# Output projections as seven quarter products in a two-layer encoder kernel

## The chip, the cores and the metric

The kernel runs on one core of a Trainium2 chip. A core has TensorE (matrix products, PE in the profile; PEld is its loading of the stationary operand), VectorE (DVE), ScalarE (ACT), GpSimd (POOL) and SyncE (SP), which here only issues DMAs. Matrix products read SBUF and write PSUM; the dense phase of this kernel keeps eight PSUM tiles of 128 x 512 fp32, here called banks. ScalarE and GpSimd issue DMAs too. Each engine runs its own instructions in program order and waits for other engines by semaphores. The metric is the device time of one execution in microseconds; lower is better.

## What is computed

The reference is a trunk of two layers over 1024 tokens of width 1024. Layer 0 mixes the tokens by neighbourhood attention (mixer A), layer 1 by grouped-query attention (mixer B). After each mixer stand the output projection, the residual sum, and a gate projection:

```python
def reference(x, p, norm_g, a_w_in, a_rpb, a_w_out, b_w_in, ..., ple_norm_g, ple_w_gate, ple_w_proj, final_norm_g):
    for i in range(DEPTH):                      # DEPTH = 2
        h = rms_norm(x, norm_g[i])
        if i % NUM_MIXERS == 0:
            y = mixer_a(h, a_w_in[j], a_rpb[j], a_w_out[j])
        else:
            y = mixer_b(h, b_w_in[j], b_q_norm[j], b_k_norm[j], b_w_out[j])
        x = x + y
        g = jax.nn.sigmoid(rms_norm(x, ple_norm_g[i]) @ ple_w_gate[i])
        x = x + g * (p[i] @ ple_w_proj[i])
    return rms_norm(x, final_norm_g)
```

Both mixers end in `(o * silu(gate)) @ w_out`, with `w_out` of 1024 x 1024. That last product, once per layer, is the output projection. In the kernel `y` names its left operand, `o * silu(gate)`.

## The kernel before, in words

**Numbers in halves.** Every fp32 operand of a product is held as two tiles of type fp32r, a high part (ScalarE's copy) and a low part (VectorE's difference). A product is three matmuls into the same PSUM bank: high x high, high x low, low x high (`split3`, L314; its matmuls stand in the profile under L315, in `mm`). A transpose is a matmul against `ident`.

**Operands.** The left operand of all dense products lies in `HTh` and `HTl`: token tile t (8 tiles of 128), channel chunk k (8 of 128), channels on the partitions. Weights come in units of 128 x 1024 fp32 (512 KB). The class `Weights` (`WQ`) keeps one queue of units: `stage` issues their loads on SP into one of two `wstage` buffers (L208), `pump`, called once per step of work, makes the high half on ScalarE (L225) and the low half on VectorE (L230, one step later). Each unit has a pool number: pool 1 has four slots that live throughout, pool 2 has four in the dense phase alone. `hold` names the unit at which staging stops, `age` and `lag` are the steps that a unit waits.

**Mixers.** Attention of 16 heads, in order, with the dense products of the next heads woven in (`mix`). `post` and `later` are lists of functions that fall due after so many steps. Two heads make a pair; when both heads of a pair are done for a token half `hf` (tiles 0 to 3, or 4 to 7), `head_end` yields `fin`: y of that pair, 128 channels x 512 tokens in the tile `Y`. For pairs 0 to 6 it is multiplied on GpSimd (L529, L530), then after `YS` = 11 steps split into halves (L526, L527), and two steps later both halves are stored to DRAM, `yD` (L522). During the last heads `load_y` (L279) brings channel chunks 0 to 6 of a tile back into `HTh` and `HTl`. The last pair goes straight there by `fin_last` (Y final at L512, halves at L515, L516). `pp_items` makes `p @ ple_w_proj` at the end of a mixer and stores it to `ppD` (L568).

**Dense phase** (`dense_phase`, L1232 on), per layer. Two kinds, `out` (output projection) and `ple` (gate projection), each for two column halves `hf` of 512, each for 8 token tiles. A tile and half is 8 chunks x 3 = 24 matmuls of 128 x 512 into one bank, written as two parts of 4 chunks. For `out` and `hf` = 0, the first parts of tiles 0 to 3 run first, since they need only pairs 0 to 3. The result is added to the residual `X` by VectorE (L1286); `X` is loaded by SP (L1344) and stays in SBUF. In the second half, each finished tile is squared and summed by ScalarE (L1369, the first half at L1360), every two tiles VectorE makes the root (`norm_r`, L426 and `rsqrt`, L326 to L334) and the scaled rows `xn` (L1382), and `pend_ht`, called once per part, transposes half a tile of them on TensorE into `HTh` and `HTl` (`to_ht`, L443 to L445) for the gate projection. There, ScalarE's tanh (L1278) and two VectorE operations (L1279, L1280) add the gated term to `X`, with `pp` tiles loaded back by SP (L1334). `rope_tables` (L1387 to L1402), called in layer 0 in the `out` half 0 at tile 4, prepares the rotary tables for mixer B: GpSimd multiplies, SP stores.

**Order of the work.** It is written out by hand: each engine runs its instructions in the order in which the Python code issues them. Nothing is reordered later; only the waits for data and for buffers are added.

## Time and profile before

| | |
|---|---|
| median of 3 runs | 1550.73 us (1549.6 to 1550.89) |
| span of the profiled execution | 1548.4 us; its whole time isn't listed apart from the runs |
| TensorE busy | 1521.1 us, 98% of the span |
| VectorE, ScalarE, GpSimd busy | 1016.2, 874.1, 280.4 us |
| output projection of layer 0 | 529.2 to 616.2 us |
| output projection of layer 1 | 1355.7 to 1442.7 us |
| moved by DMA | 138.32 MB, 89 GB/s in the mean |

How to read the lines of the profile: a group is "line, engine, operation, output <- inputs, shape, xcount | busy us, mean ns of one | idle time of the engine just before, and what ended it". A line of the timeline is "start, duration, engine, line, operation, names, xcount [idle time before it <- what ended that]"; `SPq` is a DMA's issue on SP. In the table by stretch, each engine has its busy time and its number of instructions, then come the granted TensorE clock (1.00 is full), the busy share of the DMA engines and GB/s. Matmuls are pipelined: one of 128 x 512 has a duration of some 390 ns, but the next begins after about 227.

### The profile page before, as it was taken

How to read it: one execution, taken by the hardware profiler on the slowest of the kernel's cores; microseconds unless marked ns; L12 is line 12 of the kernel's file. 1: busy time of each engine (PE TensorE's matmuls, PEld its weight loads, DVE VectorE, ACT ScalarE, POOL GpSimd, SP SyncE). 2: the span in 40 equal slices, each digit the busy share in tenths (PEclk: the TensorE clock that was granted, in tenths of full speed). 3: DMA queues.
4: the chain of work that ended last, by engine and by line, in shares of the span. 5: the costliest groups of instructions: out<-in, count | busy, mean ns of one | idle time of the engine just before them, and what ended most of it. 6: DMA issues, size and time to landing. Idle time of an engine off the chain costs nothing.

```text
span 1548.4 us, 24286 instructions
## 1 busy us (share of the span) xinstructions
PE 1521.1 (98%) x9072; PEld 1328.5 (86%) x9072; DVE 1016.2 (66%) x1990; ACT 874.1 (56%) x1757; POOL 280.4 (18%) x380
## 2 busy tenths in 40 slices
PE   8999999999999999999999999999999999999997
PEld 8888988988988888888988889989999888788886
DVE  7666576576477436557877776777777877625636
ACT  6565465465466522333567776767767767622422
POOL 1221121121121010000312122444131200000022
PEclk9999999999999999999999999999999999999999
DMA  8212122122033961232210111111101123651213
GB/s 263 97 40 72 60 80 61 52 82 79 35 99 97 355 232 55 79 139 78 75 48 22 38 48 50 41 38 56 57 27 42 62 62 116 224 197 55 74 54 131
DMA packets 90005, 138.32 MB, mean 89 GB/s; under 512 B 17056, under 2 KB 56096, under 8 KB 89888
## 3 DMA queue, kind: packets, MB, share of 16 engines
q1 hardware_dynamic: 87296, 129.17, 25.6%
q10 hardware_dynamic: 2592, 7.61, 1.4%
q8 instruction: 71, 1.16, 0.3%
q14 instruction: 46, 0.38, 0.1%
HBM read 104.13 MB, written 36.15 MB: 91 GB/s over the span
## 4 chain that ended last, share of the span: by engine, by line
PE 41%; DVE 7%; ACT 3%; issue 2%; DMA 0%; SPq 0%; ACTq 0%; DVEq 0%
PE d L315 22%; PE o L315 7%; PE t L1144 6%; PE s L315 5%; DVE PTl L1147 2%; DVE mn L1128 1%; ACT PTh L1146 1%; ACT P L1134 1%; PE t L443 1%; DVE QS L1108 1%; DVE wl L230 0%; PE t L1098 0%; DVE t L962 0%; DVE qt L963 0%; DVE Y L459 0%
## 5 line engine op out<-in xcount | busy, mean ns | idle before, releaser
L315 PE MATMUL d<-wh,HTh 128*128 128x256 f32 (+1 forms) x1096 | 369.3, 339 | 3.6 <-ACT HTh L444 1.3
L315 PE MATMUL d<-wh,HTl 128*128 128x256 f32 (+1 forms) x1096 | 363.2, 333 | 0.3 <-DVE HTl L445 0.3
L315 PE MATMUL d<-wl,HTh 128*128 128x256 f32 (+1 forms) x1096 | 362.6, 333 | 0.0
L1147 DVE TENSOR_TENSOR PTl<-t,PTh 128x512 fp32r<-128x512 f32 x256 | 164.4, 684 | 110.1 <-ACT PTh L1146 109.7
L315 PEld LDWEIGHTS d<-wh,HTh 128*128 128x128 f32 x1096 | 206.4, 189 | 26.6 <-ACT HTh L444 1.6
L315 PEld LDWEIGHTS d<-wl,HTh 128*128 128x128 f32 x1096 | 206.7, 189 | 21.7
L315 PEld LDWEIGHTS d<-wh,HTl 128*128 128x128 f32 x1096 | 206.5, 189 | 22.0 <-DVE HTl L445 0.5
L315 PE MATMUL d<-HTh,wh 128*128 128x512 f32 x504 | 205.8, 408 | 0.0
L315 PE MATMUL d<-HTh,wl 128*128 128x512 f32 x504 | 198.1, 393 | 0.0
L315 PE MATMUL d<-HTl,wh 128*128 128x512 f32 x504 | 197.5, 392 | 0.0
L1134 ACT ACTIVATE P<-s,mn 128x1024 f32<-128x1024 f32 x128 | 142.8, 1115 | 57.2 <-DVE mn L1128 56.3
L1146 ACT ACTIVATE PTh<-t 128x512 fp32r<-128x512 f32 x256 | 140.2, 594 | 45.4 <-PE t L1144 44.8
L1128 DVE TENSOR_REDUCE mn<-s 128x1 f32<-128x1024 f32 x128 | 154.8, 1209 | 11.7 <-PE s L315 11.6
L1144 PE MATMUL t<-ident,P 128*128 128x128 f32 x1024 | 137.7, 275 | 6.4 <-DVE PTl L1147 4.4
L230 DVE TENSOR_TENSOR wl<-wstage,wh 128x1024 fp32r<-128x1024 f32 x86 | 110.2, 1285 | 40.1 <-ACT wh L225 39.6
L1144 PEld LDWEIGHTS t<-ident,P 128*128 128x128 f32 x1024 | 114.6, 140 | 22.5 <-DVE PTl L1147 16.6
L315 PE MATMUL s<-KA,QS 128*128 128x512 f32 (+2 forms) x384 | 133.5, 402 | 0.0
L315 PE MATMUL s<-KB,QS 128*128 128x512 f32 (+2 forms) x384 | 121.7, 371 | 0.0
L315 PE MATMUL o<-PTh,V 128*128 128x256 f32 (+2 forms) x672 | 118.8, 288 | 1.2 <-DVE Y L459 0.9
L315 PE MATMUL o<-PTl,V 128*128 128x256 f32 (+2 forms) x672 | 119.0, 288 | 0.1
L695 DVE TENSOR_TENSOR PTl<-t,PTh 128x384 fp32r<-128x384 f32 (+1 forms) x128 | 66.6, 520 | 74.7 <-ACT PTh L694 73.4
L315 PEld LDWEIGHTS d<-HTh,wl 128*128 128x128 f32 x504 | 94.6, 188 | 21.7
(201 smaller groups left out, 2486.0 us busy)
## 6 DMA issues: line engine op xcount, KB each, us to landing
wstage<-in_wts SPq DMA_DIRECT2D x92, 512.0 KB
pp<-ppD SPq DMA_DIRECT2D x32, 256.0 KB
X<-in_x SPq DMA_DIRECT2D x15, 512.0 KB
rb<-rD SPq DMA_DIRECT2D x56, 128.0 KB
ppD<-th SPq DMA_DIRECT2D x20, 256.0 KB
xD<-X SPq DMA_DIRECT2D x8, 512.0 KB
X<-xD SPq DMA_DIRECT2D x8, 512.0 KB
yD0h<-rb SPq DMA_DIRECT2D x14, 256.0 KB
```

Source lines behind the costliest of these rows:

```text
L230: eng.tensor_tensor(lo[:, c:c + n], s[:, c:c + n], hi[:, c:c + n], ALU.subtract)
L315: pe.matmul(ps, a, b, start=first, stop=last, skip_group_check=True)
L443: pe.transpose(ps[:, k], xn[:, (4 * c + k) * 128:(4 * c + k + 1) * 128], ident)
L695: dve.tensor_tensor(PTl[:, sl], ps[:, :m], PTh[:, sl], ALU.subtract)
L1108: post.add(DQ, lambda: dve.tensor_tensor(qs[oth], raw[own], qs[own], ALU.subtract))
L1128: dve.tensor_reduce(mn, ps, axis=AX.X, op=ALU.min)
L1134: act.activation(p, ps, AF.Exp, bias=mn, scale=-1.0, accum_out=RS[h, hf][:, t:t + 1])
L1144: pe.transpose(ps[:, i], p[:, k * 128:(k + 1) * 128], ident)
L1146: act.activation(PTh[:, ks, c], ps, AF.Copy)
L1147: dve.tensor_tensor(PTl[:, ks, c], ps, PTh[:, ks, c], ALU.subtract)
```

## The change

Both output projections are made from seven products of quarter matrices instead of eight, in Winograd's form. Call the quarters of y A11 (tiles 0 to 3, chunks 0 to 3), A12 (tiles 0 to 3, chunks 4 to 7), A21, A22 (tiles 4 to 7), and of the weights B11, B12 (column halves of the first 512 rows), B21, B22. The new function `strassen_out` runs, in blocks of 12 matmuls (one tile, 4 chunks, 3 terms):

- P1 = A11 B11 (4 blocks, one for each tile), P2 = A12 B21 (4);
- S2 T2 (4), S3 T3 (4), A22 T4 (4), added onto P1 in the same PSUM banks, and read out by VectorE (`fold`) after each block;
- S1 T1 (4) and Q4 B22 (4), interleaved, in new banks.

Here T3 = B22 + B12, T2 = T3 + B11, T4 = T2 + B21, T1 = B11 + B12; S1 = A21 - A22, S3 = A11 - A21, S2 = S1 - A11, Q4 = A12 + S2. The quarters of X get their products from `fold`, `first` (P2) and `second` (P1, copied out by ScalarE) with the signs that this form needs.

The weight sums: two 512 KB tiles `SM` are loaded with B22 by SP, and GpSimd's queue issues DMAs that add B12, then B11, then B21 onto them in SBUF (`plus`), each after the halves of the sum so far are made (`wh`, `wl`). For T1 they are loaded again. The input sums are VectorE's, on fp32 quarters that SP fetches (`fetch_a`) from a new DRAM copy of y, `yF`. The mixers store it: `whole` after 11 steps, the last pair in `fin_last`. The halves `yD` are still made for tiles 0 to 3 and, of tiles 4 to 7, for chunks 4 to 6, now 4 steps after `whole`. The list `todo` says after which block each of these steps is issued.

Beside this, the gate weights of half 0 are staged only from the first block of the last eight on (`hold`), those of half 1 go to pools 4 and 2; the squares, roots and scaled rows are made in pairs of tiles (m, 4 + m) during the last eight blocks, with the buffers `sb` and the gains opened there; the gate projection's first half runs in the order 0, 4, 1, 5, 2, 6, 3, 7; and `rope_tables` moves to the end of that half.

```diff
+    yF = [dram.tile([NT, 128, 8, 128], F32, name=f"yF{l}") for l in range(2)]
...
+    WQ.hold = ("ple", 0, 0, 0)
...
-        for n in ("out", "ple"):
-            for hf in range(2):
-                q.extend([((n, l, hf, u), 1 + hf) for u in range(4)])
+        q.extend([(("out", l, 0, u), 1) for u in range(4)])
+        q.extend([(("ple", l, 0, u), 1) for u in range(4)])
+        q.extend([(("ple", l, 1, u), 4 - u // 2 * 2) for u in range(4)])
 
     def load_y(l, t):
         for d, src in zip((HTh, HTl), yD[l]):
-            (act if t < 4 else sync).dma_start(d[:, t, 0:7].bitcast(F32), src[t, :, 0:7])
+            k0 = 4 if t >= 4 else 0
+            (act if t < 4 else sync).dma_start(d[:, t, k0:7].bitcast(F32), src[t, :, k0:7])
...
+            sync.dma_start(yF[layer][ts, :, 7, :].rearrange("t p c -> p t c"), y3)
...
-            def store(c, src):
-                sync.dma_start(yD[layer][c][4 * hf:4 * hf + 4, :, pair, :].rearrange("t p c -> p t c"),
+            def store(dst, src):
+                sync.dma_start(dst[4 * hf:4 * hf + 4, :, pair, :].rearrange("t p c -> p t c"),
                                src.rearrange("p (t c) -> p t c", t=4))
 
             def split():
                 act.activation(yhi, Y, AF.Copy)
                 dve.tensor_tensor(ylo, Y, yhi, ALU.subtract)
-                post.add(2, lambda: (store(0, rb), store(1, Y)))
+                post.add(2, lambda: (store(yD[layer][0], rb), store(yD[layer][1], Y)))
+
+            def whole():
+                store(yF[layer], Y)
+                if pair >= 4 or hf == 0:
+                    post.add(4, split)
             pool.tensor_tensor(Y, Y, G, ALU.mult)
             pool.tensor_tensor(Y, Y, rb, ALU.mult)
-            post.add(YS[layer], split)
+            post.add(YS[layer], whole)
...
+    def strassen_out(l, X, ps_d, ps_t):
+        xs = x if l == 0 else xD
+        es = ExitStack()
+        scr = es.enter_context(tc.tile_pool(name="scr", bufs=1))
+        todo = {}
+
+        q11, q21 = [("out", l, 0, 0), ("out", l, 0, 1)], [("out", l, 0, 2), ("out", l, 0, 3)]
+        q12, q22 = [("out", l, 1, 0), ("out", l, 1, 1)], [("out", l, 1, 2), ("out", l, 1, 3)]
+        W = {"b11": [WQ.get(k) for k in q11], "b21": [WQ.get(k) for k in q21]}
+        SM = [scr.tile([128, 1024], F32, name=f"sum{u}") for u in range(2)]
+        raw = {}
+        P1 = [None] * 4
+        A = {n: [scr.tile([128, 4, 128], F32, name=n, bufs=4) for m in range(4)] for n in ("a21", "a22", "a11", "a12")}
+
+        def load(dst, key):
+            sync.dma_start(dst, wts[UNIT[key]])
+
+        def plus(u, keys):
+            pool.dma_start(SM[u], wts[UNIT[keys[u]]], accum_op=ALU.add)
+
+        def halves(name, u, pid, src):
+            def hi():
+                W.setdefault(name, [None, None])[u] = WQ.alloc[pid]()
+                act.activation(W[name][u][0], src(), AF.Copy)
+
+            def lo():
+                w = W[name][u]
+                dve.tensor_tensor(w[1], src(), w[0], ALU.subtract)
+            return hi, lo
+
+        H = {(n, u): halves(n, u, pid, lambda n=n, u=u: raw[u] if n == "b22" else SM[u])
+             for n, pid in (("t3", 2), ("t2", 1), ("t4", 1), ("t1", 1), ("b22", 2)) for u in range(2)}
+
+        def wh(n, u):
+            H[n, u][0]()
+
+        def wl(n, u):
+            H[n, u][1]()
+
+        def fetch_a(n, m):
+            t, c = {"a21": (4, 0), "a22": (4, 1), "a11": (0, 0), "a12": (0, 1)}[n]
+            sync.dma_start(A[n][m], yF[l][t + m, :, 4 * c:4 * c + 4])
+
+        def sums(m):
+            a21, a22, a11 = (A[n][m] for n in ("a21", "a22", "a11"))
+            dve.tensor_tensor(a22, a21, a22, ALU.subtract)
+            dve.tensor_tensor(a21, a11, a21, ALU.subtract)
+            dve.tensor_tensor(a11, a22, a11, ALU.subtract)
+
+        def q4(m):
+            dve.tensor_tensor(A["a12"][m], A["a12"][m], A["a11"][m], ALU.add)
+
+        PLACE = {"s2": ("a11", 4, 0), "s3": ("a21", 0, 0), "s1": ("a22", 0, 1), "q4": ("a12", 4, 0)}
+
+        def sh(n, m):
+            src, t, c = PLACE[n]
+            act.activation(HTh[:, t + m, 4 * c:4 * c + 4], A[src][m], AF.Copy)
+
+        def sl(n, m):
+            src, t, c = PLACE[n]
+            w = slice(4 * c, 4 * c + 4)
+            dve.tensor_tensor(HTl[:, t + m, w], A[src][m], HTh[:, t + m, w], ALU.subtract)
+
+        def first(m):
+            fold(m, 0, P2[m], ALU.add)
+
+        def second(m):
+            xt = X[m][:, 0:512]
+            dve.tensor_tensor(xt, xt, P1[m], ALU.add)
+
+        for u in range(2):
+            load(SM[u], q22[u])
+        for u in range(2):
+            plus(u, q12)
+        for n in ("a21", "a11", "a22"):
+            for m in range(4):
+                fetch_a(n, m)
+        todo[1] = [lambda: sums(0)]
+        todo[2] = [lambda: sh("s2", 0), lambda: sums(1), lambda: wh("t3", 0), lambda: wh("t3", 1)]
+        todo[3] = [lambda: sl("s2", 0), lambda: wl("t3", 0), lambda: wl("t3", 1), lambda: sh("s2", 1),
+                   lambda: plus(0, q11), lambda: plus(1, q11)]
+        todo[4] = [lambda: sl("s2", 1), lambda: sums(2)] + [lambda t=t: sync.dma_start(X[t], xs[t]) for t in range(4)]
+        todo[5] = [lambda: sums(3), lambda: sh("s2", 2), lambda: sh("s2", 3)]
+        todo[6] = [lambda: sl("s2", 2), lambda: sl("s2", 3), lambda: wh("t2", 0), lambda: wh("t2", 1)]
+        todo[7] = [lambda: wl("t2", 0), lambda: wl("t2", 1), lambda: plus(0, q21), lambda: plus(1, q21)]
+        todo[7] += [lambda m=m: fetch_a("a12", m) for m in range(4)]
+        todo[8] = [lambda: sh("s3", 0), lambda: sh("s3", 1), lambda: sl("s3", 0), lambda: sl("s3", 1)]
+        todo[8] += [lambda t=t: sync.dma_start(X[t], xs[t]) for t in range(4, 8)]
+        todo[9] = [lambda: sh("s3", 2), lambda: sh("s3", 3), lambda: sl("s3", 2), lambda: sl("s3", 3)]
+        todo[10] = [lambda: wh("t4", 0), lambda: first(0), lambda: first(1), lambda: q4(0), lambda: q4(1)]
+        todo[11] = [lambda: wh("t4", 1), lambda: wl("t4", 0), lambda: first(2), lambda: first(3)]
+        todo[12] = [lambda: wl("t4", 1), lambda: load(SM[0], q11[0]), lambda: load(SM[1], q11[1]),
+                    lambda: plus(0, q12), lambda: plus(1, q12), lambda: q4(2), lambda: q4(3)]
+        todo[13] = [lambda: sh("s1", 0), lambda: sh("s1", 1), lambda: second(0), lambda: sl("s1", 0), lambda: sl("s1", 1)]
+        todo[14] = [lambda: sh("s1", 2), lambda: sh("s1", 3), lambda: second(1), lambda: sl("s1", 2), lambda: sl("s1", 3)]
+        todo[15] = [lambda: sh("q4", 0), lambda: sh("q4", 1), lambda: second(2), lambda: sl("q4", 0), lambda: sl("q4", 1)]
+        todo[16] = [lambda: wh("t1", 0), lambda: sh("q4", 2), lambda: sh("q4", 3), lambda: second(3)]
+        todo[17] = [lambda: wl("t1", 0), lambda: wh("t1", 1), lambda: sl("q4", 2), lambda: sl("q4", 3)]
+        todo[18] = [lambda: wl("t1", 1), lambda: wh("b22", 0)]
+        todo[19] = [lambda: wl("b22", 0), lambda: wh("b22", 1)]
+        todo[20] = [lambda: wl("b22", 1)]
+
+        def fetch_raw(u):
+            raw[u] = stg.tile([128, 1024], F32, name="wstage")
+            load(raw[u], q22[u])
+        todo[14] += [lambda: fetch_raw(0), lambda: fetch_raw(1)]
+
+        def block(ps, t, c, wk, start):
+            for k in range(4):
+                wh, wl = W[wk][k // 2]
+                cc = slice((k % 2) * 512, (k % 2) * 512 + 512)
+                split3(ps, HTh[:, t, 4 * c + k, :], HTl[:, t, 4 * c + k, :], wh[:, cc], wl[:, cc],
+                       start and k == 0, k == 3)
+
+        def fold(t, c, ps, op):
+            xt = X[t][:, 512 * c:512 * c + 512]
+            if op is ALU.subtract:
+                dve.tensor_tensor(xt, xt, ps, op)
+            else:
+                dve.tensor_tensor(xt, ps, xt, op)
+
+        Y, P2 = [None] * 4, [None] * 4
+        clock = [0]
+
+        def pulse():
+            for f in todo.pop(clock[0], ()):
+                f()
+            clock[0] += 1
+
...
+        for wk, t0, c, xt0, xc, op in (("t2", 4, 0, 0, 1, ALU.subtract), ("t3", 0, 0, 4, 1, ALU.subtract),
+                                       ("t4", 4, 1, 4, 0, ALU.add)):
+            for m in range(4):
+                block(Y[m], t0 + m, c, wk, False)
+                fold(xt0 + m, xc, Y[m], op)
+                pulse()
+        WQ.live[1] += 2
+        WQ.live[2] += 2
+        for kind, m in ((5, 0), (5, 1), (3, 0), (5, 2), (3, 1), (5, 3), (3, 2), (3, 3)):
+            if kind == 5:
+                Y[m] = ps_d.tile([128, 512], F32, name="d")
+                block(Y[m], m, 1, "t1", True)
+                fold(4 + m, 1, Y[m], ALU.add)
+            else:
+                block(Y[m], 4 + m, 0, "b22", False)
+                fold(m, 1, Y[m], ALU.add)
+            pulse()
...
+            yield kind, m
...
+            ready = []
+            squared = []
+
+            def roots(n):
+                if squared and squared[0][0] < n:
+                    m = squared.pop(0)[1]
+                    sm = ss[:, 2 * m:2 * m + 2]
+                    r = sb.tile([128, 2], F32, name="rn", bufs=4)
+                    wk = sb.tile([128, 8], F32, name="wkn", bufs=2)
+                    dve.tensor_scalar(sm, sm, 0.5 / D, 0.5 * EPS, op0=ALU.mult, op1=ALU.add)
+                    rsqrt(r, sm, wk)
+                    ready.append(((m, 4 + m), r))
+
+            def scale_pair():
+                if not ready or len(pend) > 4:
+                    return
+                ts, r = ready.pop(0)
+                xs = []
+                for i, t in enumerate(ts):
+                    xn = xalloc()
+                    dve.scalar_tensor_tensor(xn, X[t], r[:, i:i + 1], g1, op0=ALU.mult, op1=ALU.mult)
+                    xs.append(xn)
+                pend.extend([(clock[0] + 3, t, xn, (c,)) for c in range(2) for t, xn in zip(ts, xs)])
+
+            for n, (step, m) in enumerate(strassen_out(l, X, ps_d, ps_t)):
+                if n == 0:
+                    sb = es.enter_context(tc.tile_pool(name="dsb", bufs=2))
+                    wp4 = es.enter_context(tc.tile_pool(name=f"wp4{l}", bufs=2))
+                    WQ.alloc[4] = lambda: [wp4.tile([128, 1024], F32R, name=f"w{c}4") for c in "hl"]
+                    WQ.cap[4] = 2
+                    WQ.hold = ("bg", 0) if l == 0 else None
+                    g1 = load_gain(sb, 2 * l + 1, 2)
+                    g2 = load_gain(sb, 2 * l + 2, 2)
+                    junk = sb.tile([128, D], BF16, name="junk", bufs=1)
+                    ss = sb.tile([128, 8], F32, name="ssn", bufs=1)
+                    WQ.age, WQ.lag, age, lag = 2, 0, WQ.age, WQ.lag
+                if step == 5:
+                    act.activation(junk, X[4 + m], AF.Square, accum_out=ss[:, 2 * m + 1:2 * m + 2])
+                else:
+                    act.activation(junk, X[m], AF.Square, accum_out=ss[:, 2 * m:2 * m + 1])
+                    squared.append((n, m))
+                WQ.pump()
+                roots(n)
+                pend_ht()
+                scale_pair()
+            WQ.age, WQ.lag = age, lag
...
+                    seq = list(range(NT)) if hf else [0, 4, 1, 5, 2, 6, 3, 7]
...
+                    order = [(t, i) for t in seq for i in range(2)]
+                    if hf == 0:
+                        order = [(t, i) for p in range(4) for i in range(2) for t in seq[2 * p:2 * p + 2]]
...
-                        if l == 0 and kind == "out" and hf == 0 and t == 4:
+                        if l == 0 and hf == 0 and t == seq[-1]:
...
+        hg = sb.tile([128, 512], F32, name="th")
         sync.dma_start(hg[:, :256], bcast(hgains, 0, 256))
+        pool.tensor_scalar(hg[:, :128], hg[:, :128], -0.125, None, op0=ALU.mult)
```

76 lines of the change are left out of this document (40 added, 36 removed).

## The prediction

> **What bounds the kernel now.** I read the page first (busy shares, the span in slices), then busy time by stretch over the two output projections, then the timelines of each engine where they begin.
>
> ```profile
> span 1548.4 us, 24286 instructions
> ...
> PE 1521.1 (98%) x9072; PEld 1328.5 (86%) x9072; DVE 1016.2 (66%) x1990; ACT 874.1 (56%) x1757; POOL 280.4 (18%) x380
> ```
> ```profile
> core 0: us, PE busy (x) PEld busy (x) DVE busy (x) ACT busy (x) POOL busy (x), PEclk, DMA share, GB/s
> 529.20:616.20 87.00, 86.92 (x395) 71.28 (x396) 43.08 (x77) 25.15 (x49) 5.50 (x4) 1.00 0.50 170
> 1355.70:1442.70 87.00, 86.94 (x395) 71.31 (x396) 37.05 (x71) 23.66 (x47) 0.00 (x0) 1.00 0.31 112
> ...
> 529.28:551.05 21.77, 21.77 (x96) 18.03 (x97) 9.38 (x11) 6.45 (x10) 0.00 (x0) 1.00 0.89 331
> 1355.76:1377.50 21.74, 21.74 (x96) 18.02 (x97) 6.25 (x7) 6.52 (x11) 0.00 (x0) 1.00 0.66 253
> ```
>
> TensorE is the bound: 98% of the span, and in both output projections (87 us each) without a gap. So removed matmuls pay in full, provided that the new operands are there in time. The price is in the third and fourth rows: 96 matmuls of 128x512 take 21.77 us, 0.227 us each. I call 12 of them (one tile, four k-chunks, three high/low terms) a block: 2.72 us.
>
> **The gain.** An output projection has 8 tiles, 2 column halves, 8 k-chunks, 3 terms: 384 matmuls, 32 blocks. Seven quarter products have 7 x 4 = 28 blocks, 336 matmuls. Over two layers 96 go, which is just the window above: -21.8 us.
>
> **Start of the Strassen stage.** P1 (A11 B11) and P2 (A12 B21) need nothing new, so they start as now and cover 8 blocks, 21.8 us. The ninth block, S2 T2, needs S2 from three fetched quarters and T2 from two accumulations in a row. When can that be?
>
> ```profile
> 529.28 0.50 PE L315 MATMUL d<-wh,HTh 128*128 128x512 f32 x1 [0.74 <-ACT G L567]
> ...
> 532.12 0.69 DVE L512 TENSOR_TENSOR Y<-Y,t 128x512 f32<-128x512 f32 x1
> 533.51 0.69 DVE L516 TENSOR_TENSOR HTl<-Y,HTh 128x512 fp32r<-128x512 f32 x1 [0.70 <-ACT HTh L515]
> 534.12 2.36 DVE L230 TENSOR_TENSOR wl<-wstage,wh 128x1024 fp32r<-128x1024 f32 x2
> ...
> 535.40 0.33 SPq L208 DMA_DIRECT2D wstage<-in_wts  x1
> 535.97 0.81 SPq L419 DMA_DIRECT2D gain<-in_gains  x2
> 536.82 1.43 SPq L1344 DMA_DIRECT2D X<-in_x  x3
> ...
> 538.91 1.06 ACT L225 ACTIVATE wh<-wstage 128x1024 fp32r<-128x1024 f32 x1 [4.48 <-DMA wstage<-in_wts]
> 544.39 0.69 DVE L1286 TENSOR_TENSOR X<-d,X 128x512 f32<-128x512 f32 x1 [3.16 <-DMA X<-in_x]
> ...
> 539.00:545.00 6.00, 6.00 (x28) 4.99 (x27) 1.83 (x2) 0.97 (x1) 0.00 (x0) 1.00 1.01 369
> 1364.00:1370.00 6.00, 6.00 (x28) 4.95 (x28) 0.31 (x1) 0.00 (x0) 0.00 (x0) 1.00 1.02 415
> ```
>
> The last pair's Y is final at 532.81, when P1 has run 3.5 us. Only then can SP store it to yF, and behind that store in SP's order stand both SM loads and twelve fetches. A lone 512 KB load lands 3.5 us after its issue (535.40 to 538.91). The fourth 512 KB of a queue lands after 9.0 us (535.40 to 544.39). With the DMA full (share 1.01, 1.02) it moves 369 to 415 GB/s. SM (1 MB), a21 and a11 (2 MB) and the first tile of a22 (0.25 MB) are 3.25 MB: 9.0 us for 2 MB and 3.5 for the rest at 369 is 12.5; at 400 GB/s behind 2.2 us of latency it is 10.7, and up to 2.7 more where the accumulations share the engines. From 533.5 that gives 544 to 547; I take T = 546.
>
> From T the new order on VectorE decides, which runs in order. A 128x512 costs 0.62 back to back (533.51 to 534.12), a 128x1024 1.18 (2.36 for two). Ahead of the first T2 low half stand four `sums` of three (2.0 each, 8.0), four `sl` of S2 (2.5), two low halves of T3 (2.4): 12.9; with that half itself 14.1. ScalarE must form S2 high and then T2 high in the same order, and ends beside it. So the ninth block starts at 560.1 where PE is ready at 551.05: 9.0 us of stall.
>
> In layer 1 the order is kinder:
>
> ```profile
> 1353.43 0.69 DVE L512 TENSOR_TENSOR Y<-Y,o 128x512 f32<-128x512 f32 x1
> ...
> 1346.31 9.75 SPq L568 DMA_DIRECT2D ppD<-th  x3
> 1358.04 0.81 SPq L419 DMA_DIRECT2D gain<-in_gains  x2
> ...
> 1355.76 0.50 PE L315 MATMUL d<-wh,HTh 128*128 128x512 f32 x1 [0.73 <-ACT th L567]
> ```
>
> Y is final at 1354.12, but SP is held by the ppD stores to 1356.1, and memory of the mixer may hold the loads to 1358.0, as it does the gains now. With 12.5 us T is 1368.6 to 1370.4; at 1369.5 the ninth block starts at 1383.6, due 1377.5: 6.1 us. Lower bound of both: a store and a fetch at 3 us each with nothing before them, T 538.9 and 1362: stalls 1.9 and 0. Upper: T 5 us later, 14 and 11.
>
> **The accumulating DMAs.** The trace has none. Nearest row: the plain load, 3.5 us; if source, destination and result each move at the plain rate behind two latencies, about 8.3. T3 low is done 5.8 after T and T2 high cannot start before 12.1, so 6.3 us are free. I take 6 (it reads and writes, so nearer the upper end): hidden. At 8.3, with a second one behind it, 3 more per layer. Not below zero: nothing else now makes these sums. Behind a late one on POOL stand only its fellows; on ScalarE, though, the P1 and S copies, and on VectorE every fold. The Trainium skill, DMA: Bandwidth & Descriptors, section Anatomy of one DMA — SWDGE (gpsimd) path, fits 2.0 us plus bytes at 436 GB/s, an estimate of 3.2 us for each; the sum would be the same by it. It is not a fit for accumulation, and no run here shows one.
>
> **Middle.** In blocks 9 to 18 VectorE has 10 folds, 12 `sl`, 4 `q4`, 8 `first`/`second` (34 x 0.62 = 21.1) and 3 `wl` (3.5): 24.6 in 27.2 us, and a fold may be three blocks late before PE waits for its bank. No cost. T4's accumulation is issued at T + 15 and needed at T + 36. T1's is tighter: SM is free again when T4 low is done, about T + 32, so load (3.5) and accumulation (6) are in at T + 42, its halves at T + 44, and PE wants them at T + 47. That holds, with 3 us to spare.
>
> **Tail into the gate projection.** Square, norm, scaling and gate weights, spread over the second column half now (half of 87 us), fall on the last eight blocks.
>
> ```profile
> 585.89 0.16 DVE L426 SCALAR_TENSOR_TENSOR stn<-sq 128x2 f32<-128x2 f32 x1 [0.85 <-ACT xn L1369]
> ...
> 588.12 2.48 DVE L1382 SCALAR_TENSOR_TENSOR xn<-X,stn,gain 128x1024 f32<-128x1024 f32 x2
> ...
> L444 ACT ACTIVATE HTh<-t 128x512 fp32r<-128x512 f32 x64 | 37.2, 593 | 47.8 <-PE t L443 47.6
> L225 ACT ACTIVATE wh<-wstage 128x1024 fp32r<-128x1024 f32 x89 | 92.9, 1051 | 9.2 <-DMA wstage<-in_wts 8.4 <-DVE HTl L516 0.8
> L736 ACT ACTIVATE junk<-X 128x1024 bf16<-128x1024 f32 x7 | 7.4, 1056 | 0.9 <-DMA X<-in_x 0.9
> L736 ACT ACTIVATION_READ_ACCUMULATOR junk<-X 128x1 f32 x7 | 1.4, 198 | 0.0
> ```
>
> A root is eleven small operations, 2.2 us (585.89 to 588.12), a pair's scaling 2.4. From the end of the fourth of the eight blocks VectorE has fold, `wl`, root, scaling (6.4), then fold and `wl` (1.8), then fold, root, scaling (5.2), then the next fold (0.6): 14.0. ScalarE's square waits for that fold (1.25), then a weight half (1.05), then HTh of tile 0 (0.6): ready at 16.9. PE has four blocks and two transpose groups to do, 11.6: stall 5.3, and about 1 more at tile 4. Take 6 per layer. Bounds 2 (if the square slips ahead) and 9 (gate weights late behind the two gain loads moved in front of them).
>
> **Clock.**
>
> ```profile
> 1540.00:1544.00 4.00, 0.21 (x2) 0.01 (x1) 3.72 (x14) 3.41 (x6) 0.00 (x0) 0.95 0.02 8
> 1544.00:1548.40 4.40, 0.00 (x0) 0.00 (x0) 0.00 (x0) 0.00 (x0) 0.00 (x0) 0.50 0.59 233
> ```
>
> After PE's last matmul, at 1540.2, the granted clock is 0.95 over four us, then 0.50: it halves after some 3.6 us of idling. The return isn't shown. If it takes one block, a stall costs 1.4 more. Both starts are well above 3.6 us, the tails (5.3) only just, so I count them as one: three, 4 us. Bounds 0 and 8. The Trainium skill, TensorE: Matmul & The Clock Gate, section Part 1: The HAM clock gate, has the same fall after about 3.4 us (the rows agree) and a return after about 3.4 us of work, an estimate of 1.7 us a stall; by it the three cost 5.
>
> **At nothing.** The yF stores (16 a layer for 8 yD stores fewer) lie under mixers whose DMA is a quarter used:
>
> ```profile
> 400.00:500.00 100.00, 99.86 (x560) 86.70 (x560) 66.35 (x143) 61.38 (x134) 19.93 (x22) 1.00 0.26 78
> ...
> 551.32 1.62 SPq L1391 DMA_DIRECT2D xn<-in_rope  x1
> 561.19 2.48 SPq L1402 DMA_DIRECT2D ropeD<-xn  x4
> ```
>
> Splits come four ticks later and VectorE's in-place half must now wait for the yF store to have read Y; 0 to 2 us in all. The shorter loads of y gain nothing, PE waits for none. The rotary tables, moved to the end of the gate's first half, hold SP some 10 us (551.32 to 561.19), and behind them the two pp loads: the first gate evacuation waits 7 us, covered by four PSUM banks (21.8 us): 0 to 2.
>
> **Sum.** -21.8 + 9.0 + 6.1 + 12 + 4 = +9.3 us. On the span that is 1557.7; the runs' median (1550.73) is 2.3 above the span, so 1560.0.
>
> **Rivals.** (1) Preparation keeps up, the other side: SP's fetches overtake or T comes 5 us earlier, and the square slips ahead in the tail. Stalls 4 + 1 + 2 x 3, no clock loss: -10.8, 1540. For it: VectorE works only 9.4 of the first 21.8 us. Against: the DMA share there is 0.89 already, while 8 MB (SM and its first two sums 3, quarters of y 3, X 2) are to come in that time. It decides where all stalls stay under 21.8 us. Chance 0.25. (2) Slow accumulations, deciding from 6.3 us each on: at 12 us T2 comes 6 us later and T1 3 us, at 15 us 9 and 6, per layer; with 13 us, +20 on the forecast, 1580. For it: they meet a DMA that is full in these stretches. Against: the plain load beside them takes 3.5. Chance 0.18. (3) Gain and stalls cancel, 1551: chance 0.07. Forecast, 1554 to 1572 of its own: 0.50.
>
> Faster by over 0.2% (3 us, what this measurement can tell) 0.25, within 0.07, slower 0.68. The range leaves a tenth out at each end: 1541 to 1580.
>
> **What would show it.** 336 matmuls for 384 in each projection; PE idle before the ninth block, released by ScalarE's or VectorE's T2 half, 9 and 6 us; T3 halves ready long before use; a second gap at the gate's first tile, released by HTh L444; granted clock under 1 behind the gaps. Wrong if the ninth block follows without a gap, or if the gap hangs on a POOL DMA.

## The result, and the profile after

The changed kernel is slower: 1597.24 us median (1595.54 to 1598.76) against 1550.16 us (1548.95 to 1550.89) for the kernel before on the same chip, a ratio of 1.0307 (95% interval 1.0292 to 1.0321). The forecast was 1560.0, with a range of 1541 to 1580: the sign was right, the size was not. The profiled execution has a span of 1594.6 us, 46.2 more than before.

First the page of the changed kernel (busy time and DMA issues), and then the group of its first-term matmuls from the answer by lines.

```profile
PE 1515.1 (95%) x8976; PEld 1317.7 (83%) x8976; DVE 1076.4 (68%) x2079; ACT 897.0 (56%) x1769; POOL 297.1 (19%) x397
...
sum<-in_wts POOLq DMA_DIRECT2D x16, 512.0 KB, 8.8
```

```profile
L317 PE MATMUL d<-wh,HTh 128*128 128x256 f32 (+1 forms) x1032 | 349.4, 340 | 45.8 <-ACT wh L1263 32.7 <-ACT HTh L446 10.3 <-ACT G L575 0.7
```

The 96 matmuls are gone (8976 for 9072), but PE is busy for 95% of a longer span and not 98%. The last line has PE's busy time and mean, and behind the second bar the idle time just before these matmuls and what ended it: 32.7 us for ScalarE's weight half at L1263, 10.3 for the transposed tile at L446. The accumulating DMA, which no trace had shown, takes 8.8 us from issue to landing.

The same idle times in order, from PE's timeline (start, duration, what ran, in brackets the idle time ahead and who ended it):

```profile
534.43 0.50 PE L317 MATMUL d<-wh,HTh 128*128 128x512 f32 x1 [0.74 <-ACT G L575]
...
573.94 0.79 PE L317 MATMUL d<-wh,HTh 128*128 128x512 f32 x1 [17.44 <-ACT wh L1263]
...
639.45 0.50 PE L317 MATMUL d<-wh,HTh 128*128 128x512 f32 x1 [4.38 <-ACT HTh L446]
715.33 0.98 PE L445 MATMUL t<-ident,xn 128*128 128x128 f32 x4 [3.86 <-DVE xn L1596]
...
1421.49 0.80 PE L317 MATMUL d<-wh,HTh 128*128 128x512 f32 x1 [15.26 <-ACT wh L1263]
...
1488.11 0.80 PE L317 MATMUL d<-wh,HTh 128*128 128x512 f32 x1 [4.37 <-ACT HTh L446]
```

The first row is the first block of layer 0: it starts at 534.43, where the kernel before had 529.28, so the first mixer has already lost 5.2 us. Then come the ninth block of layer 0 (17.44 us late), the gate (4.38), the gate's second half (3.86), and the ninth block and the gate of layer 1 (15.26, 4.37).

Behind the gaps PE is slow as well. The rows are, in this order, the first eight blocks of layer 0, the 10.88 us from the ninth block on (the time of four blocks at full speed) in layer 0, the gate's first block in layer 0, and then the stretches behind the ninth block and at the gate in layer 1:

```profile
core 0: us, PE busy (x) PEld busy (x) DVE busy (x) ACT busy (x) POOL busy (x), PEclk, DMA share, GB/s
534.43:556.20 21.77, 21.77 (x96) 17.94 (x96) 4.94 (x6) 4.68 (x7) 1.95 (x2) 1.00 0.79 236
...
573.94:584.82 10.88, 9.89 (x26) 6.73 (x27) 4.38 (x6) 4.46 (x7) 1.71 (x2) 0.61 0.86 178
...
639.45:644.16 4.71, 4.71 (x13) 3.37 (x14) 4.36 (x15) 1.63 (x3) 0.00 (x0) 0.64 0.52 185
...
1421.49:1432.37 10.88, 9.91 (x21) 6.68 (x22) 4.32 (x5) 4.59 (x7) 1.71 (x2) 0.50 0.83 168
...
1488.11:1493.40 5.29, 5.29 (x13) 4.03 (x14) 4.91 (x17) 1.63 (x3) 0.00 (x0) 0.50 0.54 196
```

Behind the ninth blocks PE completed 26 and 21 matmuls where 48 fit, at a granted clock of 0.61 and 0.50: 22 and 27 matmuls of 0.227 us, 5.0 and 6.1 us, are lost a second time. At the gates 12 matmuls (the rows count the start of one more) took 4.71 and 5.29 us where a block at full speed takes 2.72: 2.0 and 2.6 us.

With that, nearly all of the 46.2 us has a place: -21.8 for the matmuls, +5.2 in the first mixer, +32.7 in the waits ahead of the ninth blocks, +11.1 in the blocks behind them, +8.8 in the waits at the two gates, +4.6 in the slow blocks behind these, and +5.2 at the gate's second half in layer 0 (3.86 and the clock behind it; the 5.2 is what the run below that removes it gains). That makes 45.8; the remaining 0.4 us is not assigned.

### The profile page after: what moved, and what is told of

The parts are those of the page before. It is cut to its first block, busy times and chain, and to the rows that moved or that the text cites. A ratio compares the mean times of both kernels' runs of the same rounds, so it can differ in the third digit from the quotient of the medians.

```text
span 1594.6 us, 24337 instructions
## 1 busy us (share of the span) xinstructions
PE 1515.1 (95%) x8976; PEld 1317.7 (83%) x8976; DVE 1076.4 (68%) x2079; ACT 897.0 (56%) x1769; POOL 297.1 (19%) x397
## 3 DMA queue, kind: packets, MB, share of 16 engines
q0 software_dynamic: 2304, 8.39, 2.8%
## 4 chain that ended last, share of the span: by engine, by line
PE 37%; DVE 7%; ACT 4%; issue 3%; DMA 1%; POOL 0%; ACTq 0%; DVEq 0%; POOLq 0%
PE d L317 19%; PE o L317 7%; PE t L1152 6%; PE s L317 5%; DVE PTl L1155 2%; DMA sum<-in_wts 1%; DVE mn L1136 1%; ACT P L1142 1%; ACT PTh L1154 1%; DVE wl L231 1%; PE t L445 0%; DVE QS L1116 0%; PE t L1106 0%; DVE t L970 0%; DVE xn L1456 0%
## 5 line engine op out<-in xcount | busy, mean ns | idle before, releaser
L317 PE MATMUL d<-wh,HTh 128*128 128x256 f32 (+1 forms) x1032 | 349.4, 340 | 45.8 <-ACT wh L1263 32.7
L317 PE MATMUL d<-wl,HTh 128*128 128x256 f32 (+1 forms) x1032 | 342.4, 334 | 1.9 <-DVE wl L1267 1.9
L317 PE MATMUL d<-wh,HTl 128*128 128x256 f32 (+1 forms) x1032 | 342.1, 333 | 1.0 <-DVE HTl L447 1.0
L317 PEld LDWEIGHTS d<-wh,HTh 128*128 128x128 f32 x1032 | 197.5, 192 | 69.1 <-ACT wh L1263 35.1
L317 PEld LDWEIGHTS d<-wl,HTh 128*128 128x128 f32 x1032 | 197.7, 192 | 22.6 <-DVE wl L1267 3.9
L317 PEld LDWEIGHTS d<-wh,HTl 128*128 128x128 f32 x1032 | 197.5, 192 | 21.5 <-DVE HTl L447 3.2
L1136 DVE TENSOR_REDUCE mn<-s 128x1 f32<-128x1024 f32 x128 | 154.9, 1210 | 12.3 <-PE s L317 12.2
L231 DVE TENSOR_TENSOR wl<-wstage,wh 128x1024 fp32r<-128x1024 f32 x78 | 98.4, 1265 | 26.6 <-ACT wh L226 26.3
```

Source lines behind the costliest of these rows:

```text
L231: eng.tensor_tensor(lo[:, c:c + n], s[:, c:c + n], hi[:, c:c + n], ALU.subtract)
L317: pe.matmul(ps, a, b, start=first, stop=last, skip_group_check=True)
L1136: dve.tensor_reduce(mn, ps, axis=AX.X, op=ALU.min)
```

## The experiments

All kernels were patched from the changed one. Their times are of one execution each, so they are compared by stages of the trace: in the six executions whose first mixer is that of the changed kernel, the first block of layer 0 stood between 534.4 and 538.5, and a few us of the time are that alone.

### The first mixer: when the split may overwrite Y

VectorE overwrites Y with its low half, and must now wait until the yF store has read it. In the changed kernel (SP's and VectorE's rows):

```profile
192.42 0.54 SPq L525 DMA_DIRECT2D yF<-Y  x1
...
195.54 1.08 DVE L530 TENSOR_TENSOR Y<-Y,rb 128x512 fp32r<-128x512 f32 x1 [2.77 <-DMA yF<-Y]
```

The first edit gave the store 8 steps of work (ticks) instead of 4:

```diff
-                    post.add(4, split)
+                    post.add(8, split)
...
-            post.add(YS[layer], whole)
+            post.add(YS[layer] - 4, whole)
```

> The split of a pair comes 8 ticks after its yF store was issued and not 4, with the store 4 ticks earlier, so the split stands where it stood. Theory (VectorE's in-place half waits until the yF store has read Y, and the mixer's exponentials behind it run late): the first layer's projection starts near 529.5 again (534.4 with the change, 529.3 before), the wait of the split on yF<-Y is gone, and the time falls by 5 us, to 1592. Rival (the sixteen more stores load the queue whenever they stand): the start stays near 534 and the time at 1597.

It took 1598.75 us, with the first block at 535.49. The rows of this kernel say why the edit did nothing:

```profile
191.90 0.60 SPq L470 DMA_DIRECT2D rb<-rD  x1
192.60 0.54 SPq L525 DMA_DIRECT2D yF<-Y  x1
...
195.73 1.13 DVE L530 TENSOR_TENSOR Y<-Y,rb 128x512 fp32r<-128x512 f32 x1 [2.86 <-DMA yF<-Y]
```

The store was asked for earlier and went out at the same moment, 192.60: it stands in SP's order behind the loads of rb, and these wait for the row sums. The wait on the split is the same, 2.86 us. So the run neither bore out my expectation nor tested the rival; the distance in ticks was the wrong quantity. The second edit took the store out of SP's order:

```diff
             pool.tensor_tensor(Y, Y, rb, ALU.mult)
-            post.add(YS[layer], whole)
+            ts = slice(4 * hf, 4 * hf + 4)
+            pool.dma_start(yF[layer][ts, :, pair, :].rearrange("t p c -> p t c"), Y.rearrange("p (t c) -> p t c", t=4))
+            if pair >= 4 or hf == 0:
+                post.add(YS[layer], split)
```

> POOL stores yF itself, right after its last multiplication of a pair, instead of SP 11 ticks later behind its waits for the row sums, and the split stands at 11 ticks as before the change. Theory (the in-place split waits for a yF store that SP can only issue behind the loads of rb): the split's waits on yF<-Y are gone and the first projection starts at 529 to 530.5 (534.4 to 536.8 in the runs with the change, 529.3 before); the time is 1590 to 1593. Rival (the bytes or the number of the stores, wherever they are issued): the start stays at 534 or later and the time at 1596 or more.

1588.94 us. The first block starts at 529.54, as in the kernel before (529.28):

```profile
529.54 0.50 PE L317 MATMUL d<-wh,HTh 128*128 128x512 f32 x1 [0.74 <-ACT G L574]
```

VectorE's waits on `yF<-Y` in the first mixer, 3.3 us in the changed kernel, are gone. The bytes and the number of the stores are the same, so the loss of 5 us (up to 9 in other executions) did not come from them. It came with the place of the store in SP's order and with the split, which the change had put 4 ticks later; the edit takes both back, and no run separates the two.

### The start: the accumulation, the order, and where they meet

The start of layer 0 in the changed kernel, from the timelines of SP, POOL, VectorE and ScalarE:

```profile
537.99 0.37 SPq L517 DMA_DIRECT2D yF<-Y  x1
...
540.56 0.82 SPq L1255 DMA_DIRECT2D sum<-in_wts  x2
...
545.34 1.95 POOL L1258 DMA_DIRECT2D sum<-in_wts  x2 [51.89 <-DMA sum<-in_wts]
...
558.13 0.69 DVE L1285 TENSOR_TENSOR a<-a,a 128x512 f32<-128x512 f32 x1 [16.51 <-DMA a<-yF]
...
564.37 0.86 POOL L1258 DMA_DIRECT2D sum<-in_wts  x1 [17.08 <-DVE wl L1267]
...
572.83 1.06 ACT L1263 ACTIVATE wh<-sum 128x1024 fp32r<-128x1024 f32 x1 [2.26 <-DMA sum<-in_wts]
```

SP may load SM 2.6 us after the last yF store was issued. The first tile of a22 is there 17.6 us after that (558.13), and VectorE's order then puts two sums and T3's low halves ahead of the second accumulation (564.37), which lands 8.5 us later and is what the ninth block waits for. Two experiments took one link each.

```diff
-            pool.dma_start(SM[u], wts[UNIT[keys[u]]], accum_op=ALU.add)
+            pool.dma_start(SM[u], wts[UNIT[keys[u]]])
```

> The accumulating DMAs become plain copies, so the weight sums are left out (the output is not the reference's). Theory (two accumulations of 8.8 us in a row hold T2): each copy lands 3.5 to 5 us after its issue, the stall ahead of the ninth block falls from 17.4 and 15.3 us to 11 to 13 and 9 to 11, the short waits behind it go, and the time falls by 12 to 16 us, to 1581 to 1585. Rival (the quarters of y and VectorE's order alone set that moment): the stall stays above 16 us and the time within 3 us of 1597.

1586.5 us. The ninth blocks wait 13.02 and 10.79 us, 4.4 and 4.5 less. That is the upper end of what I expected (11 to 13 and 9 to 11), and the time is 1.5 us above my range: a plain copy issued by POOL in this place still takes 7.1 us and not 3.5 to 5.

```profile
556.98 0.69 DVE L1285 TENSOR_TENSOR a<-a,a 128x512 f32<-128x512 f32 x1 [13.38 <-DMA a<-yF]
...
571.50 0.80 PE L317 MATMUL d<-wh,HTh 128*128 128x512 f32 x1 [13.02 <-ACT wh L1263]
```

And from its page, DMA issues:

```profile
sum<-in_wts POOLq DMA_DIRECT2D x16, 512.0 KB, 7.1
```

SM was issued at 542.55 here, so a22 came 14.4 us later and not 17.6: accumulating, for plain copying of the same bytes, also slows the fetches, by some 3 us. What accumulating costs is this part; the greater part of the stall would be there with plain copies.

```diff
-        todo[1] = [lambda: sums(0)]
-        todo[2] = [lambda: sh("s2", 0), lambda: sums(1), lambda: wh("t3", 0), lambda: wh("t3", 1)]
-        todo[3] = [lambda: sl("s2", 0), lambda: wl("t3", 0), lambda: wl("t3", 1), lambda: sh("s2", 1),
-                   lambda: plus(0, q11), lambda: plus(1, q11)]
+        todo[1] = [lambda: wh("t3", 0), lambda: wh("t3", 1)]
+        todo[2] = [lambda: wl("t3", 0), lambda: wl("t3", 1), lambda: plus(0, q11), lambda: plus(1, q11),
+                   lambda: sums(0)]
+        todo[3] = [lambda: sh("s2", 0), lambda: sums(1), lambda: sl("s2", 0), lambda: sh("s2", 1)]
```

> T3's halves and the accumulation behind them (for T2) are issued ahead of the input sums on ScalarE, VectorE and POOL. Theory (VectorE's order: the sums of the quarters wait for the last fetch and T3's low halves stand behind them): POOL issues the accumulations for T2 near 557 instead of 564.4, the ninth block starts 6 to 8 us earlier (stall 9 to 11 us in the first layer, 8 to 10 in the second) and the time falls by 12 to 16 us, to 1581 to 1585. Rival (a full DMA: the accumulations would only move into the stretch of the fetches and take longer there, or S2 would be late instead): stall 15 us or more, time 1593 or more.

1587.81 us, between the two. In layer 0 of this kernel:

```profile
556.69 1.06 ACT L1263 ACTIVATE wh<-sum 128x1024 fp32r<-128x1024 f32 x1 [12.90 <-DMA sum<-in_wts]
...
559.31 0.86 POOL L1258 DMA_DIRECT2D sum<-in_wts  x1 [9.99 <-DVE wl L1267]
...
562.11 0.68 DVE L1285 TENSOR_TENSOR a<-a,a 128x512 f32<-128x512 f32 x1
...
572.36 1.99 ACT L1263 ACTIVATE wh<-sum 128x1024 fp32r<-128x1024 f32 x2
573.45 0.79 PE L317 MATMUL d<-wh,HTh 128*128 128x512 f32 x1 [14.88 <-ACT wh L1263]
```

Its first block was at 536.50, so POOL issues the second accumulation 22.8 us after it and not 29.9. But the ninth block gains only 2.6 us (14.88 for 17.44; 11.72 for 15.26 in layer 1): at 572.36 ScalarE no longer waits for a DMA (no bracket), it comes late because the input sums, which now start at 562.11, stand ahead of it. Two chains of about equal length end at the ninth block, the weight sums and the input sums; shortening one shows the other. That is why neither run alone came near the 9 and 6 us that I had forecast.

### The clock behind the gap

```diff
+        zero = scr.tile([128, 128], F32R, name="zero")
...
+        for _ in range(62):
+            mm(Y[0], zero, W["b21"][1][0][:, 0:512], False, False)
         for wk, t0, c, xt0, xc, op in ...
```

> Ahead of the ninth block PE runs 62 matmuls with a zero operand, 14.1 us at full speed, in place of most of its idling; the operands come no sooner. Theory (the gap itself costs 17.4 and 15.3 us, and the granted clock halves behind it for about 8 us of the next work, some 3 us of loss in each layer): the ninth block starts at the same distance from the first (39.5 and 37.3 us), the clock is full behind it, and the time falls by 4 to 8 us, to 1589 to 1593. Rival (the slow start of blocks 9 to 12 is only the late second halves of T2): less than 2 us, 1595 or more.

1596.69 us, with the first block at 538.51. By stretches, layer 0 and then layer 1 of this kernel:

```profile
560.28:577.88 17.60, 14.36 (x65) 11.56 (x63) 12.82 (x19) 5.85 (x8) 1.71 (x2) 1.00 1.04 358
577.88:588.76 10.88, 9.56 (x27) 6.60 (x28) 4.63 (x6) 4.20 (x6) 1.71 (x2) 0.69 0.89 183
...
1409.66:1424.47 14.81, 14.34 (x64) 11.54 (x63) 11.71 (x18) 5.85 (x8) 1.71 (x2) 1.00 1.05 357
1424.47:1435.35 10.88, 8.24 (x33) 6.04 (x33) 5.94 (x8) 4.20 (x6) 1.71 (x2) 1.00 0.86 186
```

In layer 1 the fill left a gap of 0.48 us; the clock stayed at 1.00, 33 matmuls and not 21 went through in the next 10.88 us, and the gate came 63.95 us after the ninth block and not 66.62: 2.7 us for the clock. The other 15 of the 48 are missing at full clock too, so more than half of the 6.1 us there is late second halves of T2. In layer 0 the fill left a gap of 3.24 us, the clock halved all the same (1.0 us behind the gap, when one matmul had run), and little was gained (27 matmuls for 26). So both readings hold a part, and for layer 0 the shares stay open.

### The gate's second half and the tails

```diff
-                        if l == 0 and hf == 0 and t == seq[-1]:
-                            rope_tables(sb)
...
                     load_pp(0)
                     load_pp(1)
+                    if l == 0 and hf == 1:
+                        rope_tables(sb)
```

> In the first layer the first two pp loads of the gate's second half are issued ahead of the rotary tables and not behind them. Theory (the tables hold SP, the first gate evacuation waits for its pp tile, and PE for the bank): the 3.9 us wait of the transposes near 715 and the 3.4 us at half clock behind it go, 5 to 6 us in all, to 1591. Rival (the tables would then delay the stores of x behind them, with PE waiting there): the time stays at 1596 to 1597.

1592.91 us. No wait above 0.3 us is left between the first gate block (642.10) and the next mixer's first wait, a 0.6 us one that all kernels have (751.62): 109.5 us, where the changed kernel takes 114.7 (639.45 to 754.17). 5.2 us, as the theory said.

```diff
+                pend_ht()
                 if step == 5:
                     act.activation(junk, X[4 + m], AF.Square, accum_out=...)
...
                 WQ.pump()
                 roots(n)
-                pend_ht()
                 scale_pair()
```

> In the last eight blocks the transposes of the normed tiles and their evacuation are issued ahead of the block's square on ScalarE, and not behind it. Theory (ScalarE's evacuation of the first tile stands behind a square that waits for a fold, and that fold on VectorE behind a root and a scaling): the wait of 4.4 us at the first gate block goes in both layers, with the half clock behind it, and the time falls by 8 to 12 us, to 1585 to 1589. Rival (VectorE has too much to do there in any order, and the next operand is late instead): a wait of 3 us or more stands at one of the first four gate blocks, and the time is 1593 or more.

1596.67 us, with the first block at 538.24. PE's rows in layer 0:

```profile
640.85 0.50 PE L317 MATMUL d<-wh,HTl 128*128 128x512 f32 x1 [1.83 <-DVE HTl L447]
649.47 0.50 PE L317 MATMUL d<-wh,HTl 128*128 128x512 f32 x1 [1.97 <-DVE HTl L447]
```

The 4.4 us wait for ScalarE is gone in both layers, and two waits for VectorE's low halves, 3.8 us together, stand in its place. From the ninth block on, layer 0 is 1.2 us shorter (to the mark at the next mixer) and layer 1 4.1 us (to the end). The rival had the larger part in layer 0, my theory in layer 1.

### The edits together, and a wait that gave the gain back

The next kernel has four of the edits at once: the POOL stores, T3's chain first, the tables behind the pp loads, the transposes ahead of the squares.

> Four of the edits together: yF stored by POOL, T3's halves and T2's accumulation ahead of the input sums, the rotary tables behind the pp loads, and the transposes of the last blocks ahead of the squares. Theory (these are separate losses, one behind the other on PE's path): they add up, 5 to 8 us in the first mixer, 6 to 9 at the two starts, 5 at the gate of the first layer, 4 to 6 at the two tails, to 1571 to 1578; what is left above the kernel before is the two starts, where the ninth block still waits 10 us or more. Rival (they share one cause, and a gain at one place is given back at the next): 1582 or more.

1578.76 us, just above my range and below the rival's: they did not quite add up. The mixer's gain is there (first block at 531.31) and is given back at once: the ninth block of layer 0 waits 19.95 us, longer than ever, and starts at 573.33 as in the kernel with T3's chain alone (573.45). Two rows of it, SP's and POOL's:

```profile
537.67 0.82 SPq L1254 DMA_DIRECT2D sum<-in_wts  x2
...
547.24 1.83 POOL L1257 DMA_DIRECT2D sum<-in_wts  x2 [54.56 <-DMA a<-yF]
```

POOL starts the accumulations 9.6 us after the plain loads were issued, where it took 4.8 in the changed kernel. The kernel with the POOL stores alone does so too (535.88 to 545.39). What is new in the DMA view of these two kernels in this place is one row; it stands here for 545.4 to 545.6 of the kernel with the four edits:

```profile
q14 instruction: 1, 0.01, 9.7%
```

A packet of an instruction queue crosses there, after 2.3 MB of loads and fetches that the DMA moved since 537.67, and POOL goes on 1.8 us later. The next kernel adds 28 empty writes on POOL early in the mixer, so that its code lies otherwise:

```diff
+            for _ in range(2 if layer == 0 else 0):
+                pool.memset(spot, 0.0)
             ts = slice(4 * hf, 4 * hf + 4)
```

> The four edits together once more, with 28 empty writes of one column on POOL, spread over the first mixer, so that POOL's later instructions lie 28 places further on in its code. It is to tell why, in the first layer, the kernels with the POOL stores begin their accumulations 9.5 to 10 us after the plain loads were issued (545.4 and 547.2), where the others take 4.6 to 4.8, which gave the mixer's gain back. Theory (POOL had to fetch its next instructions there, and a packet of an instruction queue does cross the DMA 1.6 to 1.9 us before POOL goes on in each of the three kernels that show it and in none of the others; it lay behind 3 MB of fetches): with the code shifted POOL goes on 4.5 to 5.5 us after the issue, the ninth block starts 5 us earlier (14 to 15.5 us of stall and not 20), 1572 to 1575. Rival (the plain loads themselves land late there): POOL again at 545 to 547.5, 1577 or more.

1573.02 us.

```profile
536.91 0.82 SPq L1257 DMA_DIRECT2D sum<-in_wts  x2
...
541.63 1.83 POOL L1260 DMA_DIRECT2D sum<-in_wts  x2 [49.79 <-DMA sum<-in_wts]
...
567.50 0.80 PE L318 MATMUL d<-wh,HTh 128*128 128x512 f32 x1 [14.87 <-ACT wh L1265]
```

POOL goes on 4.7 us after the issue, the wait is 14.87 us again, and the ninth block comes 36.9 us after the first and not 42.0. Work that does nothing made the kernel 5.7 us faster. That speaks against the rival (loads that land late): the loads were not touched and were issued 6.4 us after the first block in both kernels. The last kernel below has the same empty writes, and there POOL goes on 4.6 us after the issue. With this the edits give 24 us of the 47 back, and the two starts (14.87 and 11.39 us) are the main rest.

### Another order of the products

S3 T3 needs no late column of y and one accumulation only. Two kernels put it third, ahead of S2 T2, so that 10.9 us of work stands where the gap was. The core of the first (T4 is formed from the staged copy of B21, T1 as T2 minus B22, by POOL):

```diff
-        for wk, t0, c, xt0, xc, op in (("t2", 4, 0, 0, 1, ALU.subtract), ("t3", 0, 0, 4, 1, ALU.subtract),
-                                       ("t4", 4, 1, 4, 0, ALU.add)):
+        for wk, t0, c, folds in (("t3", 0, 0, ()), ("t2", 4, 0, ((0, 1, ALU.subtract), (4, 1, ALU.subtract))),
+                                 ("t4", 4, 1, ((4, 0, ALU.add),))):
```

> Three of those edits (not the order of T3), and another order of the products: S3 T3 third, since it needs the first half of y's columns and one accumulation only, then S2 T2, then A22 T4; T4 is formed by VectorE from the fp32 copy of B21 that still lies in its staging buffer, and T1 by POOL as T2 minus B22, so that four accumulating DMAs a layer are left of eight. Theory (the loss at the start is how long after the first block T2 and S2 can be ready, near 33 to 37 us in any order, and 10.9 us of other work put ahead of them hides most of it): waits ahead of the third, fourth and fifth product below 3 us each, no long half clock, 1538 to 1550, so about the kernel before or up to 0.8% faster. Rival (VectorE, with four more folds and two more sums a layer, is then the bound, and the middle and the tail wait for it): 1552 to 1565.

1588.33 us: the gap ahead of the third product fell (4.68 us in layer 0, 0.8 in layer 1), and the loss moved behind it, to VectorE, beyond even the rival's number. Rows of layer 1 of this kernel, POOL's and VectorE's:

```profile
1404.95 3.38 POOL L1300 TENSOR_TENSOR a<-a,a 128x512 f32<-128x512 f32 x2 [1.51 <-DVE a L1297]
1405.57 3.31 DVE L1314 TENSOR_TENSOR HTl<-a,HTh 128x512 fp32r<-128x512 f32 x2
...
1414.14 6.95 POOL L1325 TENSOR_TENSOR X<-X,P 128x512 f32<-128x512 f32 x4 [1.23 <-DVE X L1384]
...
1416.42 1.27 DVE L1384 TENSOR_TENSOR X<-d,X 128x512 f32<-128x512 f32 x2
1417.62 2.34 DVE L1270 TENSOR_TENSOR wl<-sum,wh 128x1024 fp32r<-128x1024 f32 x1
```

A pair of low halves takes 3.31 us beside POOL's additions (1.29 without), a weight half 2.34 (1.22), while a pair of folds, which reads one operand from PSUM, takes 1.27 as ever. The second kernel has no arithmetic on POOL:

```diff
+        for m in range(4):
+            Z[m] = ps_t.tile([128, 4, 128], F32, name="t").rearrange("p k c -> p (k c)")
+            block(Z[m], m, 0, "t3", True)
+            pulse()
+        for wk, c, folds in (("t2", 0, ((0, 1, ALU.subtract), (4, 1, ALU.subtract))), ("t4", 1, ((4, 0, ALU.add),))):
```

> The order S3 T3, S2 T2, A22 T4 again, now with no arithmetic on POOL beside VectorE: S3 T3 goes into the banks of the second product (P1 + P2 is formed in the copy of P1 and added to X by an accumulating DMA), T1 is summed by DMAs in the tiles of a21, the other sums go back to VectorE, and in the tail a scaling comes one block later. Theory (in the earlier kernel with this order VectorE's pairs of low halves took 3.3 us and not 1.3 wherever POOL added, so VectorE was the bound by that contention; without it it has some 62 us of work for 76): waits of 2 us or less ahead of each product in the second layer, 3 to 6 in all in the first, 1536 to 1549, as fast as the kernel before or faster. Rival (VectorE's work itself is too much, or the accumulations come late in this order too): 1552 or more.

1566.66 us, the best of these, and still 1% above the kernel before (1551.63 beside it). The gaps at the starts are gone (0.57 and 0.53 us ahead of the third product), and the clock is nearly whole. What is left are thirteen waits of 0.3 to 3.2 us in each layer, ten and eleven of them released by VectorE; the longest, 3.12 and 3.15 us, is for a weight half of ScalarE, which had itself waited for sums of VectorE. One stretch of layer 1, while the fifth product ends:

```profile
1420.00:1431.00 11.00, 8.53 (x35) 6.22 (x34) 10.90 (x19) 4.31 (x8) 0.00 (x0) 1.00 0.23 42
```

VectorE is busy for 10.90 of 11.00 us here, and PE for 8.53. The extra operands cost VectorE more than this stretch has; the rival's first half is right. None of these kernels is below the kernel before.

## Why the prediction was wrong

**The gain** is right: 96 matmuls, -21.8 us.

**The start** is the step that failed. It said T, the landing of the first tile of a22, at 16.7 us after the first block in layer 0 and 13.7 in layer 1, and 14.1 us from T to the ninth block. Measured, T is at 23.7 (558.13) and 21.4 us, 7.0 and 7.6 later, beyond my upper bound of 5; from T to the ninth block it is 15.8 and 15.9, only 1.7 later. 9.0 + 7.0 + 1.7 = 17.7 and 6.1 + 7.6 + 1.8 = 15.5: the chain on VectorE was counted right, and the two stalls of 17.4 and 15.3 follow from T. What put T late is what the accumulations take of the DMA that they share with the fetches, a term that I had let be 0 to 2.7 us; in T = 546 it is nothing, since 12.5 us is the time of the plain loads alone.

SM's loads were issued 1.9 us later than I had them, in both layers (6.1 us after the first block for 4.2, and 3.1 for 1.2): SP's wait there is put down to the last yF store. From that issue to T it took 17.6 and 18.2 us, 5.1 and 5.7 more than the 12.5. The DMA queues in that stretch of layer 0 (540.56 to 558.13), and as the last row POOL's queue in the run with plain copies (542.55 to 556.98):

```profile
q1 hardware_dynamic: 1833, 3.87, 63.2%
q0 software_dynamic: 288, 1.05, 30.3%
...
q0 software_dynamic: 288, 1.05, 18.3%
```

A row has packets, MB and the share of the 16 engines' time; q0 holds POOL's DMAs. The first two accumulations took 30.3% of 17.57 us, 5.3 us of all engines (29.1% of 18.22 us, again 5.3, in layer 1), and plain copies of the same bytes 2.6 us. What is left, 12.3 and 12.9 us, is the 12.5 of the plain loads: these were priced right. That the 5.3 us stand in T in full is an estimate from these shares; the run with plain copies shows 3.1 of them, which is about the difference between 5.3 and 2.6.

**The accumulating DMA** took 8.8 us, above my bounds (3.5 to 8.3) and above the 6.3 us that I called free, so the second one ended the chain (2.26 us of ScalarE's wait at 572.83). Yet rival (2), slow accumulations, is only a part: with plain copies 10.7 of the 37 us between forecast and result come back. The estimate of 3.2 us for a DMA of this size, from the fit of the Trainium skill (DMA: Bandwidth & Descriptors, Anatomy of one DMA — SWDGE (gpsimd) path), which I had said is not one for accumulation, doesn't hold here for plain copies on that path either: they took 7.1 us.

**The clock** was put at 4 us in all for three stalls; the blocks behind the two starts alone lost 5.0 and 6.1, of which the run with the zero operand gives 2.7 to the clock in layer 1. The slow blocks behind the gates lost 2.0 and 2.6 more. The step that let the return take one block (2.72 us) failed: after work had begun again at the two starts the clock stayed at half for the time of three blocks and more.

```profile
573.94:582.10 8.16, 7.17 (x14) 4.55 (x15) 2.98 (x3) 4.19 (x6) 1.71 (x2) 0.50 0.92 196
582.30:584.82 2.52, 2.52 (x13) 2.05 (x12) 1.20 (x3) 0.27 (x1) 0.00 (x0) 0.99 0.61 117
1421.49:1431.90 10.41, 9.44 (x20) 6.30 (x21) 4.32 (x5) 4.19 (x6) 1.71 (x2) 0.50 0.86 176
1432.40:1440.00 7.60, 7.60 (x35) 6.26 (x34) 5.75 (x10) 3.95 (x7) 0.00 (x0) 1.00 0.01 2
```

It came back 8.4 and 10.8 us after the first matmul, with PE busy for about 90% of that time. The rule that I had cited, a return after some 3.4 us of sustained work (the Trainium skill, TensorE: Matmul & The Clock Gate, What's actually happening), is not what these rows show as long as PE pauses in between. Where PE ran without a pause the clock was back 3.5 us (behind 715.33) and 5.6 us (behind 1488.11) after the first matmul.

The fall was not at one length of idling. My 3.6 us were counted from the start of the row; from PE's last matmul, at 1540.2, they are 3.4. At the two starts of the changed kernel the clock fell 2.0 and 2.1 us after PE's last matmul (at 558.5 and 1408.4), and at the gate's second half 4.0 us after it. In layer 0 with the fill it fell 1.0 us behind a gap of 3.24 us, when one matmul had run; a gap of 0.48 us in layer 1 did not bring it down. The same section of the Trainium skill puts the fall at about 3.4 us of idling; the kernel before agrees, and the starts, at 2.0 and 2.1 us, do not.

**The tails** were put at 6 us each and are 4.4, at the place and by the releaser forecast. That the square stands ahead of the transposed tile was right; moving it showed VectorE behind it, as the sum over VectorE's steps had it.

**At nothing** I had put the yF stores (0 to 2 us, 5.2 measured) and the tables (0 to 2, 5.2 measured). In both the edit was seen and its cover was overrated: VectorE's in-place half waits for a store that stands behind other waits in SP's order, and the four PSUM banks did not last until the two pp tiles were there. **The middle** cost nothing, as said.

So the sign came from the stalls, as forecast, and the 37 us that were missing are the two starts (17.6), the clock and the late second halves behind starts and gates (15.7 where I had 4, so 11.7), the mixer and the tables (10.4), less 3.2 at the tails; 0.4 on the span is not assigned.

## What to carry to other kernels

Price a transfer with everything that the change itself puts into the same stretch of the DMA, and not by a row from a quieter place: here 17.6 us stood where the plain loads alone gave 12.5, and 5.3 of them were the accumulations. Where two chains end at the same matmul, an experiment on one shows little; ask of each how late it is alone. And a new store or load costs what stands ahead of it in its queue: the same store cost 5 us of the first mixer on SP, behind waits, and nothing there on POOL.
